# Batched 64x64 matrix multiplication: the second half of six `a` tiles' transposes moved ahead of the multiplication it used to follow

## The chip, the cores and the metric

The kernel runs on one core of a Trainium2 chip. The metric is the device time of one execution in microseconds (us); lower is better. Next to it the profile gives a span, from the first to the last instruction, which is here about 1.8 us shorter than the time.

## The reference, cut to what matters

```python
a = np.random.randn(1024, 64, 64).astype(np.float32)
b = np.random.randn(1024, 64, 64).astype(np.float32)
out = np.matmul(a, b).astype(np.float32)
```

Each of the three tensors has 1024 x 64 x 64 x 4 bytes = 16.8 MB. The kernel reads two of them and writes one, 50.3 MB, each byte once.

## The kernel before

The work is cut into 8 tiles of `a` (index s, 128 products each) and 16 tiles of `b` and of the output (index t, 64 products each); tile t uses half of `a` tile t // 2. The steps concerned here, and the engines that do them:

- `regroup(s)`: VectorE casts and reorders the loaded `a` tile to bf16.
- `transpose(s, j)`: TensorE transposes half j of it (8 transposes), ScalarE copies the results from PSUM, the memory that TensorE writes, into `at_sb` (2 copies).
- `spread(t)`: VectorE spreads `at_sb`, which must hold both halves j, into a block-diagonal matrix `at_bd` (4 copies).
- `cast(t)`: VectorE casts the `b` tile to bf16, `b_bf`.
- `multiply(t)`: TensorE runs 64 matmuls, and ScalarE (for odd t VectorE too) evicts, that is copies, 8 pieces of PSUM into `o_sb` (16 smaller ones of the last tile).
- `store(t)`: GpSimd issues the transfer of `o_sb` to memory, one tile later than its multiplication.

```python
    def transpose(s, j):
        a_cols = abf_tiles[s][:].rearrange("p v h k -> p v (h k)").bitcast(fp32)
        for wl in range(2):
            at_ps = t_psum.tile([128, 4, 128], fp32, name="at_ps")
            for vo in range(4):
                nc.tensor.transpose(
                    at_ps[:, vo, :], a_cols[:, 4 * vo + 2 * j + wl, :], identity[:]
                )
            nc.scalar.copy(
                at_tiles[s][:, j, :, wl, :, :],
                at_ps[:].rearrange("p vo (g mp) -> p g mp vo", mp=4),
            )
    # ... cut: spread, cast, the body of multiply ...
        if last:
            held[t] = [lambda q=q: put(2 * q, 2) for q in range(4)]
        else:
            whole = t < n_t - 2
            held[t] = [lambda q=q: put(q, 8 if whole else 4) for q in ([0] if whole else [0, 4])]
    # ... cut: the start ...
        for t in range(n_t):
            s, half = t // 2, t % 2
            if t + 1 < n_t:
                spread(t + 1)
                cast(t + 1)
            if t + B_AHEAD < n_t:
                load_b(t + B_AHEAD)
            if half == 0 and 0 < s < n_s - 1 - A_AHEAD:
                load_a(s + 1 + A_AHEAD)
            multiply(t)
            if t == 0:
                regroup(1)
                load_a(A_AHEAD)
                load_a(A_AHEAD + 1)
                transpose(1, 0)
            elif t == 1:
                regroup(2)
            elif half == 0 and s + 2 < n_s:
                regroup(s + 2)
            if half == 0 and s + 1 < n_s:
                transpose(s + 1, 1)
            if half == 1 and s + 2 < n_s:
                transpose(s + 2, 0)
            if t >= HOLD - 1:
                store(t - HOLD + 1)
```

The order of these lines is the order in which each engine gets its instructions.

## Time and profile before

| | before |
|---|---|
| time, median of 3 | 135.64 us (135.61 to 135.66) |
| span of the profiled run | 133.8 us |
| busiest compute engine | VectorE, 93.9 us, 70% |
| bytes between memory and core | 50.3 MB, 376 GB/s over the span |
| last eviction ends | 123.67 us |
| VectorE's waits for the transposed copies | 15.1 us in 6 waits |

The profile is read from two sides. The page says which resource is occupied over the whole span. The timeline says what each engine does and, in brackets, how long it had idled before and what ended that. Here is one place of the timeline of the kernel before, with start and duration in us ahead of engine and line: the transposes of the second half on TensorE, and ScalarE around them.

```profile
57.11 1.44 PE L115 MATMUL at_ps<-identity,a_bf 128*128 128x128 f32 x8
...
59.78 0.58 ACT L172 COPY o_sb<-o_ps 64x512 f32<-64x512 f32 x1
...
60.39 1.07 ACT L118 COPY at_sb<-at_ps 128x512 f32<-128x512 f32 x2
...
61.35 3.56 ACT L172 COPY o_sb<-o_ps 64x512 f32<-64x512 f32 x6
```

TensorE is done with the transposes at 58.55. ScalarE copies them out (line 118) only at 60.39, since the evictions (line 172) of the multiplication written before them come first. VectorE's spread, which starts at 61.50, waited for that.

### The profile page before, as it was taken

The numbers are of one execution on the slowest core, as the hardware profiler recorded it, in microseconds if no ns is written. First come the engines' busy times: TensorE is split into PE (matmuls) and PEld (weight loads), VectorE is DVE, ScalarE is ACT, GpSimd is POOL, SyncE is SP. The second block draws the span as 40 slices with busy tenths as digits, with TensorE's granted clock in tenths as the row PEclk, the third lists the DMA queues.
The fourth block names the chain that finished last, engine by engine and source line by source line (L and its number), as shares of the span: only waits on it lengthen the run. The fifth ranks groups of instructions, "written<-read, shape, count | busy, mean of one in ns | idle before, by whom it ended". The sixth has DMA issues, their size and how long they took to land.

```text
span 133.8 us, 2832 instructions
## 1 busy us (share of the span) xinstructions
PE 65.8 (49%) x1152; PEld 61.6 (46%) x1152; DVE 93.9 (70%) x120; ACT 87.7 (66%) x161; POOL 37.4 (28%) x49
## 2 busy tenths in 40 slices
PE   0005505990078524976398276839535860974000
PEld 0005305990078513966396266738525750963000
DVE  5920299208997039998998999999889949979000
ACT  3134504999137994399779979967994999498000
POOL 8981000420082150307023021404200430426400
PEclk9999999999558965589658977977997798555555
DMA  3999999999999999999999999999999999999991
GB/s 75 359 335 312 305 315 312 306 304 305 306 307 384 365 310 310 393 391 396 317 306 355 403 388 371 318 301 374 393 390 391 393 396 404 404 387 356 337 334 51
DMA packets 17485, 45.01 MB, mean 336 GB/s; under 512 B 1088, under 2 KB 1088, under 8 KB 17472
## 3 DMA queue, kind: packets, MB, share of 16 engines
q0 software_dynamic: 7440, 22.28, 54.8%
q1 hardware_dynamic: 5520, 13.11, 27.0%
q10 hardware_dynamic: 4512, 9.44, 18.6%
q8 instruction: 9, 0.15, 0.4%
q14 instruction: 4, 0.03, 0.1%
HBM read 33.55 MB, written 16.78 MB: 376 GB/s over the span
## 4 chain that ended last, share of the span: by engine, by line
DMA 35%; SPq 27%; ACT 10%; issue 8%; DVE 7%; POOL 3%; PE 3%; POOLq 1%; ACTq 1%; DVEq 0%
SPq L72 23%; DMA a_raw<-in_a_dram 18%; DMA b_sb<-in_b_dram 17%; ACT o_sb L172 8%; DVE at_bd L128 4%; SPq L91 3%; POOL out_dram L161 3%; DVE b_bf L139 3%; PE o_ps L184 3%; ACT at_sb L118 2%; SPq L85 1%; ACT b_bf L146 1%; POOLq L277 1%; ACTq L91 1%; POOLq L161 0%
## 5 line engine op out<-in xcount | busy, mean ns | idle before, releaser
L172 ACT COPY o_sb<-o_ps 64x512 f32<-64x512 f32 x106 | 61.6, 581 | 15.6 <-PE o_ps L184 14.4
L184 PEld LDWEIGHTS <-at_bd 128*128 128x128 bf16 x1024 | 42.8, 114 | 38.0 <-DVE b_bf L139 27.3
L184 PE MATMUL o_ps<-b_bf,at_bd 128*128 128x64 bf16 x960 | 41.2, 214 | 33.3 <-DVE b_bf L139 24.5
L128 DVE COPY at_bd<-at_sb 32x1024 f32<-32x1024 f32 x64 | 45.7, 714 | 16.8 <-ACT at_sb L118 15.1
L161 POOL DMA_DIRECT2D out_dram<-o_sb x20 | 20.3, 1018 | 62.0 <-ACT o_sb L172 24.8
L115 PE MATMUL at_ps<-identity,a_bf 128*128 128x128 f32 x128 | 23.2, 346 | 21.9 <-ACT a_bf L100 11.5
L115 PEld LDWEIGHTS at_ps<-identity,a_bf 128*128 128x128 f32 x128 | 19.7, 184 | 22.1 <-issue 19.3
L118 ACT COPY at_sb<-at_ps 128x512 f32<-128x512 f32 x32 | 17.5, 590 | 8.2 <-PE at_ps L115 7.9
L68 POOL DMA_DIRECT2D a_sb<-in_a_dram x21 | 13.0, 634 | 25.2 <-DVE a_bf L103 19.4
L139 DVE CAST b_bf<-b_sb 128x2048 bf16<-128x2048 f32 x14 | 17.9, 1277 | 1.1 <-DMA b_sb<-in_b_dram 0.7
L172 DVE COPY o_sb<-o_ps 64x512 f32<-64x512 f32 x14 | 9.7, 690 | 0.3
L106 DVE CAST a_bf<-a_raw 128x1024 bf16<-128x1024 f32 x7 | 4.8, 687 | 6.3 <-DMA a_raw<-in_a_dram 6.3
L103 DVE COPY a_bf<-a_sb 128x3072 bf16<-128x3072 bf16 x7 | 6.7, 952 | 0.0
L100 ACT CAST a_bf<-o_sb 128x1024 bf16<-128x1024 f32 x2 | 2.1, 1044 | 5.5 <-DMA o_sb<-in_a_dram 5.5
L139 ACT CAST b_bf<-b_sb 128x2048 bf16<-128x2048 f32 x1 | 1.9, 1898 | 4.0 <-DMA b_sb<-in_b_dram 4.0
L100 DVE CAST a_bf<-o_sb 128x1024 bf16<-128x1024 f32 x2 | 2.5, 1249 | 2.6 <-DMA o_sb<-in_a_dram 2.6
L172 DVE COPY o_sb<-at_ps 64x256 f32<-64x256 f32 x8 | 3.4, 422 | 1.0 <-PE at_ps L184 0.9
L184 PE MATMUL at_ps<-b_bf,at_bd 128*128 128x64 bf16 x64 | 3.6, 242 | 1.0 <-DVE at_bd L128 1.0
L212 DVE MEMSET at_bd<- 128x4096 f32 x1 | 3.5, 3472 | 0.8 <-issue 0.8
L172 ACT COPY o_sb<-at_ps 64x256 f32<-64x256 f32 x8 | 2.9, 367 | 0.1
L209 ACT ACT_TABLE_LOAD x1 | 1.3, 1283 | 2.3 <-issue 2.3
L217 POOL MEMSET at_bd<- 128x2048 f32 x1 | 1.8, 1849 | 0.0
(12 smaller groups left out, 5.6 us busy)
## 6 DMA issues: line engine op xcount, KB each, us to landing
out_dram<-o_sb POOLq DMA_DIRECT2D x14, 1024.0 KB, 22.9
a_sb<-in_a_dram POOLq DMA_DIRECT2D x21, 256.0 KB, 17.8
a_raw<-in_a_dram SPq DMA_DIRECT2D x7, 512.0 KB, 24.1
o_sb<-in_a_dram ACTq DMA_DIRECT2D x2, 512.0 KB, 7.4
o_sb<-in_a_dram SPq DMA_DIRECT2D x2, 512.0 KB, 6.3
out_dram<-o_sb POOLq DMA_DIRECT2D x2, 512.0 KB, 9.4
out_dram<-o_sb POOLq DMA_DIRECT2D x4, 256.0 KB, 8.1
b_sb<-in_b_dram SPq DMA_DIRECT2D x8, 0.5 KB, 22.0
```

Of the source, the lines that this page charges most:

```text
L68: nc.gpsimd.dma_start(out=a_sb[:, h, :, :].rearrange("p v k -> p (v k)"), in_=a_v[s, h])
L72: nc.sync.dma_start(out=a_raw[:].rearrange("p v k -> p (v k)"), in_=a_v[s, 3])
L91: queue.dma_start(out=b_sb[:], in_=b_v[t])
L103: nc.vector.tensor_copy(a_bf[:, :, 0:3, :], cast_sb[:].rearrange("p h v k -> p v h k"))
L106: nc.vector.tensor_copy(a_bf[:, :, 3, :], raw[:])
L115: nc.tensor.transpose(at_ps[:, vo, :], a_cols[:, 4 * vo + 2 * j + wl, :], identity[:])
L118: nc.scalar.copy(at_tiles[s][:, j, :, wl, :, :], at_ps[:].rearrange("p vo (g mp) -> p g mp vo", mp=4),)
L128: nc.vector.tensor_copy(bd[rows, :, :, :, h, :].rearrange("p j g wl mo -> p j (g wl) mo"), at_tiles[t // 2][rows, :, half, :, :, :].rearrange(
L139: (nc.vector.tensor_copy if t else nc.scalar.copy)(b_bf[:], b_sb[:])
L161: nc.gpsimd.dma_start(out=o_v[t, :, lo : lo + n, :], in_=o_sb[:, lo : lo + n].rearrange("p gh j wl n -> p (gh j wl n)"),)
L172: copies[2 * par + wl](dst, src)
L184: nc.tensor.matmul(o_ps[:, gl, g % 2, j, :], at_bd[:, j, g, :, u], b_bf[:, g, 64 * u : 64 * u + 64], start=(u == 0), stop=(u == 1),)
```

## The change

The intent is to have the transposed copies ready earlier: for s from 1 to 6 `transpose(s + 1, 1)` is written before `multiply(2s)`, so ScalarE copies it out ahead of that multiplication's eight evictions, and VectorE's next spread has nothing to wait for.

```diff
             if half == 0 and 0 < s < n_s - 1 - A_AHEAD:
                 load_a(s + 1 + A_AHEAD)
+            if half == 0 and 0 < s < n_s - 1:
+                transpose(s + 1, 1)
             multiply(t)
             if t == 0:
                 regroup(1)
                 load_a(A_AHEAD)
                 load_a(A_AHEAD + 1)
                 transpose(1, 0)
+                transpose(1, 1)
             elif t == 1:
                 regroup(2)
             elif half == 0 and s + 2 < n_s:
                 regroup(s + 2)
-            if half == 0 and s + 1 < n_s:
-                transpose(s + 1, 1)
```

## The prediction

> **What bounds the kernel now.** I read the page's busy shares and 40 slices first, then its table of DMA queues, then the timeline, then transfers window by window at the end of the span.
>
> ```profile
> PE 65.8 (49%) x1152; PEld 61.6 (46%) x1152; DVE 93.9 (70%) x120; ACT 87.7 (66%) x161; POOL 37.4 (28%) x49
> ...
> DMA  3999999999999999999999999999999999999991
> ...
> q0 software_dynamic: 7440, 22.28, 54.8%
> q1 hardware_dynamic: 5520, 13.11, 27.0%
> q10 hardware_dynamic: 4512, 9.44, 18.6%
> ...
> HBM read 33.55 MB, written 16.78 MB: 376 GB/s over the span
> ```
>
> No compute engine passes 70% of the span, while the 16 DMA engines show 9 in every slice but the first and last. The three large queues' packet times sum to 54.8 + 27.0 + 18.6 = 100.4% of 16 engines' span: there was a packet in hand practically always. These bytes are fixed: 1024 x 16 KB x 3 tensors = 50.3 MB. So transfers bound the whole, unless they are only busy because compute feeds them exactly as fast as they drain. That I settle at the end of the span, where a bound by compute would show as DMA engines running dry before the last stores.
>
> The chain of waits that ended last puts 35% on DMA and 27% on SyncE's issuing, mostly `a_raw` loads held in the issuer for over 10 us each; that too looks like full queues. But seen from the engines alone, the middle of the kernel looks like VectorE's:
>
> ```profile
> 49.50:61.40 11.90, 8.71 (x145) 8.08 (x145) 11.09 (x15) 7.81 (x16) 2.08 (x2) 0.65 1.05 365
> 61.40:73.40 12.00, 8.17 (x147) 7.54 (x143) 11.22 (x14) 10.22 (x21) 3.86 (x6) 0.72 1.06 337
> 73.40:84.80 11.40, 7.09 (x138) 6.50 (x135) 11.03 (x15) 10.23 (x21) 2.35 (x3) 0.85 1.04 380
> ```
>
> Columns: window, length, then busy time of PE, weight loads, DVE, ACT and POOL, the granted clock, DMA share and GB/s. One `a` tile (two multiplications) takes about 11.8 us, of which VectorE works 11.1. So VectorE paces the computing there, and the change speaks to just that pace.
>
> One `a` tile moves 3 x 2.1 = 6.3 MB. At the 376 GB/s of the page that is 16.7 us, more than the 11.8 us of compute. So in this stretch compute gains on the transfers; loads are ahead, and what lags is stores, held in 8 output buffers. The debt falls due at the end:
>
> ```profile
> 117.00:121.00 4.00, 3.05 (x58) 2.89 (x56) 3.02 (x6) 3.89 (x8) 1.10 (x2) 0.50 1.03 386
> 121.00:125.00 4.00, 0.85 (x16) 0.69 (x13) 2.57 (x7) 2.35 (x7) 3.12 (x5) 0.50 1.01 353
> 125.00:130.00 5.00, 0.00 (x0) 0.00 (x0) 0.00 (x0) 0.00 (x0) 0.15 (x1) 0.50 0.99 334
> 124.00:134.00 10.00, 0.00 (x0) 0.00 (x0) 0.00 (x0) 0.00 (x0) 1.15 (x2) 0.50 0.67 231
> ```
>
> After 124.0 no compute engine does anything; stores alone run for another 8 us or so.
>
> **What the skill says.** The Trainium skill's "DMA: Bandwidth & Descriptors", section "Issuing engines are not separate DMA queues", says that transfers started by any engine end on the same 16 DMA engines and interleave. The sum of 100.4% agrees. "Perfetto Trace Analysis", section "Identifying the Most-Contended Engine", warns that occupancy of 16 DMA engines misleads and asks for HBM utilization; section "Roofline" takes 358 GB/s as a core's share and about 435 GB/s as what the 16 engines of a core alone can do. The measured 376 lies between, 86% of the latter; slices reach 404. So the engines are not at the page's ceiling, and a little better mixing could be worth something, but the queues never empty. "TensorE: Matmul & The Clock Gate", section "Architectural detail: the array is 16× 32×32, not 1× 128×128", says ScalarE and VectorE are strict FIFO and TensorE pulls only weight loads ahead. Hence moving lines really moves execution. The trace agrees: ScalarE's transposed copies at 60.39 us run after the evictions written before them.
>
> **The change, part by part.** It adds and removes no instruction. For s = 1 to 6 it puts 8 PE transposes and their 2 ScalarE copies before multiplication 2s. At t = 0 the two transposes stay adjacent and in their place, so nothing changes there. Moved in all: 48 transposes and 12 copies. A batch of 8 transposes took 1.07 to 1.97 us in the timeline; two copies 2 x 0.59 = 1.18 us (1.07 as merged).
>
> What it should win: after multiplication 2s VectorE goes through spread and cast for 2s+1 and the regrouping of a later tile, then the spread for 2s+2, which needs both halves of the transposed tile. Today the second half is copied behind all eight evictions:
>
> ```profile
> 61.50 2.83 DVE L128 COPY at_bd<-at_sb 32x1024 f32<-32x1024 f32 x4 [0.58 <-ACT at_sb L118]
> ...
> 73.44 2.83 DVE L128 COPY at_bd<-at_sb 32x1024 f32<-32x1024 f32 x4 [0.40 <-ACT at_sb L118]
> ...
> 97.04 2.83 DVE L128 COPY at_bd<-at_sb 32x1024 f32<-32x1024 f32 x4 [0.58 <-ACT at_sb L118]
> ...
> 109.30 3.10 DVE L128 COPY at_bd<-at_sb 32x1024 f32<-32x1024 f32 x4 [1.72 <-ACT at_sb L118]
> ```
>
> The brackets are VectorE's idle time: 0.58 + 0.40 + 0.58 + 1.72 = 3.28 us. At 84.78 there is no such wait, and earlier long ones (15.76, 30.47) belong to tiles that the change doesn't touch. With the copies early, all four should vanish.
>
> What it costs: the 2 copies stand ahead of the eight evictions of 2s. But ScalarE idles there now: 0.93, 3.34, 1.56, 0.95, 1.88 and 1.87 us before the evictions at 41.22, 55.63, 67.57, 78.91, 91.17 and 103.43 in the timeline, waiting for PE. The six holes sum to 10.5 us; the six pairs of copies need 6 x 1.1 = 6.6 and fit nearly everywhere. PE has room as well: it waits 2.0 to 4.0 us for the cast `b_bf` before each even multiplication. So the copies are mostly hidden and computing gains at most 3.3 us, likely 2 to 3. Part of it is doubtful: at 100.54 VectorE waits 0.67 us for a `b` load, so what is won earlier is then in part waited for again.
>
> On the end of the span: from 117 us on the trace moved 4.94 MB. Stores 14 and 15, 2.10 MB, were not yet issued at 117.0 (first piece 118.29). So 4.94 - 2.10 = 2.84 MB were already queued, 7.4 us at that window's 386 GB/s. Compute that comes 3 us earlier adds to a queue that lasts 7 us; **the expected share on the path is nearly nothing**. What can be left is mixing: stores alone ran at 334 GB/s from 125 to 130 us, against a mean of 395 from 100 to 112 us, while loads ran along. If 2 to 3 us of compute turn 1 MB of store from the first to the second, 1.05/0.334 - 1.05/0.395 = 0.49 us; I take half, since loads would be displaced and the slow tail looks tied to the smaller last pieces: 0.24 us. So 135.64 - 0.24 = 135.4 us.
>
> **Rivals.**
> 1. VectorE bounds, and its waits count in full: 135.64 - 3.28 = 132.4 us, 2.4% faster. For it: 11.1 of 11.8 us busy. Against: 2.84 MB queued at 117 us, and 8 us of stores alone after compute.
> 2. A new wait on ScalarE or PE: all six pairs of copies delay evictions in full, 6 x 1.18 = 7.1 us later compute. For it: ScalarE is busy 10.2 of 11.8 us. The queue at the end covers up to about 7 us, so even that gives at most 136 to 137. Against: the holes listed above. A subtler version is the clock: batches of 64 matmuls take 2.04 us after short gaps and 3.59 after long ones, and moving transposes away lengthens the gap before odd multiplications. It costs 1.5 us of PE, which has slack.
> 3. Transfers are hidden anyway and simply reorder: earlier stores compete with loads of `b`, VectorE waits for those. Time stays within 0.5 us of before. This is close to what I predict; it differs in showing growing DMA waits on VectorE.
>
> **Range and chances.** Runs before lie within 0.05 us, so noise is small. Below, rival 1 in part (a third of 3.28 us) gives 134.5; above, a worse packing or delayed loads 0.5 us, to 136.1. Faster by over 2% needs under 132.9, nearly the whole of rival 1: 3%. Slower by over 2% needs over 138.4, more than rival 2 gives: 1%.
>
> **What would show it.** DMA stays at 9 in all middle slices and the queues still sum to about 100%. VectorE's waits for `at_sb` fall by about 3 us from 61 us on; ScalarE's idle before even evictions shrinks by about 1 us each. Compute's last eviction comes 1 to 3 us before the present 123.7, and the time from it to the end grows by as much. I am wrong if the span shrinks as much as compute does (then queued stores weren't the bound), if the GB/s of the tail change by over 5%, or if compute ends later.

## The result, and the profile after

The changed kernel is correct and takes 135.48 us in the median of 4 runs (135.40 to 135.87), beside 135.62 us for the kernel before (135.51 to 135.66). The ratio is 0.9996, with a 95% interval of 0.9976 to 1.0017: the same time. Ratios here and below are the mean time of one kernel's runs over that of the other's runs of the same rounds, so they are not quite the ratios of the medians quoted.

The profiled span is 133.8 us, as before. On the page, the DMA row, the three queues' lines and the bytes are as they were. What changed is inside. The timeline of the changed kernel, at the place that answers to the one shown of before, and at the four spreads that the prediction listed with waits of 0.58, 0.40, 0.58 and 1.72 us:

```profile
48.97 1.97 PE L115 MATMUL at_ps<-identity,a_bf 128*128 128x128 f32 x16 [1.30 <-DVE a_bf L106]
...
50.13 2.05 ACT L118 COPY at_sb<-at_ps 128x512 f32<-128x512 f32 x4
...
54.14 4.74 ACT L172 COPY o_sb<-o_ps 64x512 f32<-64x512 f32 x8 [1.96 <-PE o_ps L184]
...
60.49 2.84 DVE L128 COPY at_bd<-at_sb 32x1024 f32<-32x1024 f32 x4
...
71.89 3.08 DVE L128 COPY at_bd<-at_sb 32x1024 f32<-32x1024 f32 x4
...
95.35 3.21 DVE L128 COPY at_bd<-at_sb 32x1024 f32<-32x1024 f32 x4
...
107.00 3.09 DVE L128 COPY at_bd<-at_sb 32x1024 f32<-32x1024 f32 x4
```

All 16 transposes of a tile now run in one batch, ScalarE copies all four results in one go before the evictions, and none of the four spreads has a bracket any more. The aim of the change is met. Two lines each of the table of waits show what became of it (who waited for whom: us in total, times, longest). The kernel before:

```profile
DVE at_bd L128 <- ACT at_sb L118: 15.1, 6, 6.3
...
DVE b_bf L139 <- DMA b_sb<-in_b_dram: 0.7, 1, 0.7
```

The changed kernel:

```profile
DVE at_bd L128 <- ACT at_sb L118: 11.6, 2, 6.0
...
DVE b_bf L139 <- DMA b_sb<-in_b_dram: 2.6, 4, 1.5
```

VectorE waits 3.5 us less for the copies (the four waits, 3.28 us, are gone; the two that stay belong to the start). It waits 1.9 us more for loads of `b`. So over half of what was won was waited for again, on transfers, in this pair of profiles. In two further pairs told below (whole stores, two queues) the copies gave back 3.7 and 3.0 us, and the waits for `b` grew by 1.1 and 0.5 us only.

One such wait matters most. It stands between the third of the four spreads and the fourth. The kernel before:

```profile
100.54 1.23 DVE L139 CAST b_bf<-b_sb 128x2048 bf16<-128x2048 f32 x1 [0.67 <-DMA b_sb<-in_b_dram]
```

The changed kernel:

```profile
100.06 1.23 DVE L139 CAST b_bf<-b_sb 128x2048 bf16<-128x2048 f32 x1 [1.50 <-DMA b_sb<-in_b_dram]
```

The changed kernel started its third spread 1.69 us ahead of the kernel before (95.35 and 97.04), but this cast only 0.48 us ahead, and the fourth spread 2.30 us ahead (107.00 and 109.30). In the two other pairs the lead at this cast was -0.28 and 0.09 us, and 1.84 and 1.54 us at the fourth spread. So a load of `b` that comes at about 100 us in either order takes back what the earlier moves won, and the lead at the end is the last move's. Of the 1.69 us in the pair shown, 0.73 were there at 48.8 us already, ahead of all four waits, since an `a` load landed earlier (VectorE waited 5.71 us for it and not 6.26); the two other pairs had 0.04 and 0.03 us there.

The end of computing, the last evictions on VectorE and ScalarE. The kernel before:

```profile
120.18 3.49 DVE L172 COPY o_sb<-at_ps 64x256 f32<-64x256 f32 x8 [0.91 <-PE at_ps L184]
120.40 3.03 ACT L172 COPY o_sb<-at_ps 64x256 f32<-64x256 f32 x8
```

The changed kernel:

```profile
117.59 3.49 DVE L172 COPY o_sb<-at_ps 64x256 f32<-64x256 f32 x8 [0.22 <-PE at_ps L184]
118.34 3.03 ACT L172 COPY o_sb<-at_ps 64x256 f32<-64x256 f32 x8
```

Start plus duration gives the end: 123.67 us before, 121.37 us after, 2.3 us sooner in this profile. The windows of the changed kernel that answer to those in the prediction (window, length, busy PE, weight loads, DVE, ACT, POOL, granted share of TensorE's full clock, packets' time as a share of the 16 DMA engines', GB/s):

```profile
117.00:121.00 4.00, 1.49 (x52) 1.37 (x47) 3.67 (x9) 3.86 (x10) 1.77 (x4) 1.00 1.03 384
121.00:125.00 4.00, 0.00 (x0) 0.00 (x0) 0.08 (x1) 0.37 (x1) 1.99 (x3) 0.65 1.00 343
125.00:130.00 5.00, 0.00 (x0) 0.00 (x0) 0.00 (x0) 0.00 (x0) 0.00 (x0) 0.50 0.99 343
```

The compute columns empty earlier, the last two columns stay: a DMA share of 1.03, 1.00 and 0.99, beside 1.03, 1.01 and 0.99 before. The time from the last eviction to the end of the span grew from 10.1 to 12.4 us, by exactly what computing gained.

### The profile page after: what moved, and what is told of

Same layout as the page of the kernel before. It is cut to its first block, busy times and chain, and to the rows that moved or that the text cites. A ratio compares the mean times of both kernels' runs of the same rounds, so it can differ in the third digit from the quotient of the medians.

```text
span 133.8 us, 2832 instructions
## 1 busy us (share of the span) xinstructions
PE 65.7 (49%) x1152; PEld 62.7 (47%) x1152; DVE 94.6 (71%) x120; ACT 87.7 (66%) x161; POOL 38.5 (29%) x49
## 4 chain that ended last, share of the span: by engine, by line
DMA 35%; SPq 27%; DVE 15%; issue 6%; ACT 3%; POOL 3%; PE 3%; POOLq 1%; DVEq 0%; ACTq 0%
SPq L72 22%; DMA a_raw<-in_a_dram 18%; DMA b_sb<-in_b_dram 17%; DVE at_bd L128 8%; DVE b_bf L139 5%; SPq L91 3%; POOL out_dram L161 3%; PE o_ps L184 3%; ACT o_sb L172 2%; DVE o_sb L172 1%; SPq L85 1%; ACT b_bf L146 1%; DVE a_bf L106 1%; DVE a_bf L103 1%; POOLq L278 1%
## 5 line engine op out<-in xcount | busy, mean ns | idle before, releaser
L184 PEld LDWEIGHTS <-at_bd 128*128 128x128 bf16 x1024 | 41.6, 111 | 34.9 <-DVE b_bf L139 22.4
L184 PE MATMUL o_ps<-b_bf,at_bd 128*128 128x64 bf16 x960 | 41.9, 215 | 31.1 <-DVE b_bf L139 20.9
L128 DVE COPY at_bd<-at_sb 32x1024 f32<-32x1024 f32 x64 | 46.0, 719 | 13.4 <-ACT at_sb L118 11.6
L115 PEld LDWEIGHTS at_ps<-identity,a_bf 128*128 128x128 f32 x128 | 21.6, 196 | 20.8 <-issue 19.3
L118 ACT COPY at_sb<-at_ps 128x512 f32<-128x512 f32 x32 | 16.9, 596 | 8.2 <-PE at_ps L115 8.0
L68 POOL DMA_DIRECT2D a_sb<-in_a_dram x21 | 13.9, 673 | 25.9 <-DVE a_bf L103 19.9
L139 DVE CAST b_bf<-b_sb 128x2048 bf16<-128x2048 f32 x14 | 17.4, 1245 | 2.9 <-DMA b_sb<-in_b_dram 2.6
L106 DVE CAST a_bf<-a_raw 128x1024 bf16<-128x1024 f32 x7 | 5.5, 792 | 5.7 <-DMA a_raw<-in_a_dram 5.7
L184 PE MATMUL at_ps<-b_bf,at_bd 128*128 128x64 bf16 x64 | 2.0, 193 | 1.2 <-DVE at_bd L128 1.2
## 6 DMA issues: line engine op xcount, KB each, us to landing
out_dram<-o_sb POOLq DMA_DIRECT2D x4, 256.0 KB, 10.1
```

Of the source, the lines that this page charges most:

```text
L68: nc.gpsimd.dma_start(out=a_sb[:, h, :, :].rearrange("p v k -> p (v k)"), in_=a_v[s, h])
L106: nc.vector.tensor_copy(a_bf[:, :, 3, :], raw[:])
L115: nc.tensor.transpose(at_ps[:, vo, :], a_cols[:, 4 * vo + 2 * j + wl, :], identity[:])
L118: nc.scalar.copy(at_tiles[s][:, j, :, wl, :, :], at_ps[:].rearrange("p vo (g mp) -> p g mp vo", mp=4),)
L128: nc.vector.tensor_copy(bd[rows, :, :, :, h, :].rearrange("p j g wl mo -> p j (g wl) mo"), at_tiles[t // 2][rows, :, half, :, :, :].rearrange(
L139: (nc.vector.tensor_copy if t else nc.scalar.copy)(b_bf[:], b_sb[:])
```

## The experiments

The theory is that transfers set the end: they are in hand all the time, and computing that ends sooner only lengthens the queue of stores. The rivals are that VectorE's chain sets the end and the change gained nothing for it, or that something new took the gain. The first pair lightens the transfers, the delays load the computing, and the last runs look at the tail.

### Less to store: does the order of the transposes matter then?

Tiles 0 to 13 store only half of each tile, in both kernels. The output is wrong (the unwritten half makes the error undefined); computing is untouched.

```diff
-            held[t] = [lambda q=q: put(q, 8 if whole else 4) for q in ([0] if whole else [0, 4])]
+            held[t] = [lambda q=q: put(q, 4) for q in ([0] if whole else [0, 4])]
```

> The kernel before, with only half of each of the first 14 output tiles stored (wrong output on purpose): 14 x 0.52 = 7.3 MB of 50.3 MB less to move, computing untouched. Theory (queued transfers set the end): the time falls well below 135.6 us, to where computing and a short last store set it, about 123 to 127 us (computing now ends at 123.7 of a span of 133.8, and its DMA waits shrink). Rival (VectorE's chain sets the end even now): the time hardly moves, above 133 us.

> The changed kernel with the same half stores. Theory: once transfers no longer set the end, the order of the transposes shows: 1.5 to 3.3 us faster than the kernel before with half stores (computing ended 2.3 us sooner in the changed kernel, 3.28 us of waits on the transposed copies are gone). Rival (what the waits on copies gave is taken back by waits on loads of b or by slower PE batches): within 0.5 us of the kernel before with half stores.

Measured: 130.73 us for the order before (ratio to the kernel before 0.9642, interval 0.9600 to 0.9684) and 127.90 us for the changed order (0.9433, interval 0.9379 to 0.9487). The first lies 3.7 us above the range that I had expected, as computing itself became no faster: its last eviction came at 123.01 us, beside 123.67 with all stores, and the span went on for another 6.8 us of last stores. The second is 2.8 us faster than the first, and the intervals do not touch. So the same change that is worth nothing in the full kernel is worth about 2.2% where transfers leave it room. The DMA and GB/s rows of the 40 slices show that room. The order before with half stores:

```profile
DMA  3999999999999999999999999999999934222790
GB/s 72 357 341 309 309 312 316 307 304 296 320 307 340 334 309 331 390 351 290 319 390 352 311 305 383 393 407 371 347 331 339 335 147 167 77 87 83 249 313 9
```

The changed order with half stores:

```profile
DMA  3999999999999999999999999999999998043790
GB/s 56 361 353 305 306 312 322 306 308 285 317 304 310 375 306 310 374 391 302 293 353 389 336 313 314 385 392 398 396 376 307 365 324 319 4 170 123 243 310 1
```

Toward the end of both rows the DMA engines fall to 0 to 4 tenths before the last stores come. Here the last stores wait for computing. In the full kernel, before and after the change, there is no such dip.

### One of the six moves alone

With half stores and the order before, only `transpose(7, 1)` is moved, ahead of multiplication 12.

```diff
+            if t == 12:
+                transpose(s + 1, 1)
             multiply(t)
...
-            if half == 0 and s + 1 < n_s:
+            if half == 0 and s + 1 < n_s and t != 12:
                 transpose(s + 1, 1)
```

> The kernel before with half stores (wrong output on purpose), and only the last of the six moves made (at tile 12). The kernel before with half stores waited 2.31 us for the copies there and 2.06 us at four earlier places. If the waits add up as they stand, this gains about 2 us of the 2.8 us (128.3 to 129.3 us) and the earlier five moves the rest. If the earlier moves carry the gain, it stays near 130.5 us.

Measured: 128.10 us, ratio 0.946, which can't be told from the 0.9433 of all six moves. So the last move carries nearly the whole gain: 130.73 - 128.10 = 2.6 us by the medians (2.5 us by the ratios, which is the fairer comparison of runs from different rounds and chips), about the 2.31 us for which VectorE had waited there, within the spread of these runs (127.61 to 129.36). What became of the five others can be read from the waits of VectorE. With the last move alone:

```profile
DVE at_bd L128 <- ACT at_sb L118: 13.6, 5, 6.2
...
DVE o_sb L172 <- ACT o_sb L172: 0.6, 1, 0.6
...
DVE b_bf L139 <- DMA b_sb<-in_b_dram: 0.2, 1, 0.2
```

With all six moves:

```profile
DVE at_bd L128 <- ACT at_sb L118: 11.8, 2, 6.2
...
DVE b_bf L139 <- DMA b_sb<-in_b_dram: 1.6, 1, 1.6
DVE o_sb L172 <- ACT o_sb L172: 1.0, 1, 1.0
```

The earlier moves save 13.6 - 11.8 = 1.8 us of waiting for copies, and 1.4 us more are waited for a load of `b`, 0.4 us more for an eviction: 1.8 us again, in these two profiles. The early part of the gain was traded mostly for a transfer even here; the last move comes after that wait, and no load takes it back.

### Computing made later

Idle VectorE memsets of a 128x1024 scratch tile are put into one iteration of the loop, 3 or 10 of them, at tile 13.

```diff
     warm = consts.tile([128, 2], fp32)
+    idle = consts.tile([128, 1024], fp32)
...
             s, half = t // 2, t % 2
+            if t == 13:
+                for _ in range(10):        # 3 in the run with 3
+                    nc.vector.memset(idle[:], 0.0)
```

> The changed kernel with 3 idle VectorE memsets (about 2.6 us by the 3.47 us of the 128x4096 memset) ahead of tile 13's work. Theory: the stores queued at the end hide it, time within 0.4 us of the changed kernel. Rival (the last computing sets the end): 2.6 us slower, about 138.1 us.

> The changed kernel with 10 such memsets, about 8.7 us. Theory: the queue covers some 6 us (last piece landed near 131.9, its issue ended near 123.1, an unqueued piece needs some 2.5 us), so the rest, 2 to 4 us, shows: 137.5 to 139.5 us. Rival: the full 8.7 us, 144 us.

> The kernel before with the same 10 memsets. Theory: it lacks the 2.3 us by which computing ended sooner, and here, where the queue has run dry, that shows: 1.5 to 3 us slower than the changed kernel with 10 memsets. Rival (the change gained nothing that lasts): within 0.5 us of it.

A memset took 0.91 us plus 0.28 us to the next, so 10 of them are 11.9 us and not 8.7. The range expected for 10 was therefore too low: with 11.9 the same sum gives 135.5 + 11.9 - 6 = 141.4 us. Measured: with 3 memsets the changed kernel takes 135.55 us (ratio 0.9997, interval 0.9980 to 1.0014), though its last eviction came at 124.73 us, 3.4 us later than without them and later than in the kernel before. With 10 memsets it takes 140.80 us, and the kernel before with 10 takes 141.06 us. The last eviction with 3 memsets:

```profile
121.24 3.49 DVE L173 COPY o_sb<-at_ps 64x256 f32<-64x256 f32 x8 [0.88 <-PE at_ps L185]
```

The run with 3 is the plainest evidence for the theory: 3.4 us of later computing cost nothing. The other two give a size of what is hidden. In the changed kernel the last eviction moved from 121.37 to 132.93, 11.6 us, and the time rose by 140.80 - 135.48 = 5.3; 6.2 us were hidden. In the kernel before it moved from 123.67 to 133.27, 9.6 us, and the time rose by 141.06 - 135.62 = 5.4; 4.2 us were hidden. The difference of 2.1 us confirms nothing: both sums start from the last evictions without memsets, so the 2.3 us between those are in it by construction. These are sums over single profiles.

The expected gap of 1.5 to 3 us between the two was missed: it is 0.26 us, which lies in the range set down for the rival. The experiment was badly placed: the memsets at tile 13 sit right where VectorE waited 1.72 us for the copies in the kernel before, and filled that wait (its waits for the copies were 12.9 us there and not 15.1). Before that wait there was hardly a lead to show: the memsets started at 107.42 us in the changed order and at 107.76 in the order before. So I put them one tile later.

### The same delay one tile later

```diff
-            if t == 13:
+            if t == 14:
```

> The kernel before with the 10 memsets (11.9 us as measured) one tile later, where they can't fill VectorE's 1.72 us wait ahead of tile 14's spread. Theory: the last eviction moves to about 135.6 us of the span and, with the queue run dry, the span ends some 6 us after it (6.0 and 6.0 in the two first delay runs), so about 143.5 us. Rival (the change gained nothing that lasts, and the 0.26 us between the first two delay runs is all there is): within 0.5 us of the changed kernel with the same delay.

> The changed kernel with the same later memsets. Theory: last eviction near 133.1 us, about 141.1 us in all, 1.8 to 2.7 us faster than the kernel before with them. Rival: within 0.5 us of it.

Measured: 141.03 us for the order before (ratio 1.0408, interval 1.0377 to 1.0440) and 140.55 us for the changed order (1.0349, interval 1.0315 to 1.0384). The expected 143.5 us and the expected difference both failed. The time after the last eviction was 4.4 us and not 6, because tile 14's store had been issued before the delay and only 1 MB was left. And the difference is 0.5 us with intervals that overlap, not 2: in these profiles the memsets started at 114.86 (order before) and 114.71 us (changed order), so at this point the changed kernel had almost no lead at all. As worded, the rival (within 0.5 us) came true in both placings: under these delays the change gained nothing that lasts. That its gain can last where there is room, only the runs with half stores show.

Multiplication 13 shows where the lead had gone. TensorE's timeline has it in the kernel before as

```profile
107.64 2.04 PE L184 MATMUL o_ps<-b_bf,at_bd 128*128 128x64 bf16 x64 [1.24 <-DVE b_bf L139]
```

in the changed kernel as

```profile
107.15 2.45 PE L184 MATMUL o_ps<-b_bf,at_bd 128*128 128x64 bf16 x64 [2.43 <-DVE b_bf L139]
```

and in the changed order with whole last stores (an experiment told below) as

```profile
107.56 3.59 PE L184 MATMUL o_ps<-b_bf,at_bd 128*128 128x64 bf16 x64 [3.20 <-DVE b_bf L139]
```

In five profiles with the transposes in their old place and all stores, this batch of 64 matmuls took 2.04 us, after TensorE had idled 0.45 to 1.35 us. In six with them moved ahead it took 2.45 to 3.60 us, after 2.42 to 3.20 us of idling, as nothing stands between multiplications 12 and 13 there any more; the granted clock from 106 to 112 us was 0.89 to 1.00 in the five of the first kind, and 0.50 to 0.72 in the six of the second. In the changed kernel with the later memsets it took 3.30 us; ScalarE then waited 1.84 us for the first matmuls, and VectorE 1.21 us for ScalarE's evictions of the same tile:

```profile
109.45 3.55 ACT L173 COPY o_sb<-o_ps 64x512 f32<-64x512 f32 x6 [1.84 <-PE o_ps L185]
...
113.04 1.39 DVE L173 COPY o_sb<-o_ps 64x512 f32<-64x512 f32 x2 [1.21 <-ACT o_sb L173]
```

In the order before with these memsets, the spread ahead of them started at 108.80 us and VectorE's eviction at 113.19; here they started at 107.39 and 113.04. So a lead of 1.4 us had shrunk to 0.15. The lead at the last eviction was 2.3, 0.6 and 1.1 us in the three pairs of full kernels profiled (plain, whole stores, two queues). I did not run a kernel that changes the idling alone, so that the idling causes the lower clock is not shown. It fits the run with whole stores, where the clock was 1.00 from 105 to 106 us and 0.50 from 107 on. It does not fit the run with 3 memsets, where the clock was 0.50 from 103 us on, before the idling, and stayed there. Nor is the idle time a measure of the clock: the last batch of the kernel before took 3.59 us after only 0.95 us of idling, that of the same order with two queues 2.04 us after 0.90.

### The tail: whole stores

The last two tiles are stored in one piece of 1 MB each, in both orders.

```diff
-            held[t] = [lambda q=q: put(2 * q, 2) for q in range(4)]
+            held[t] = [lambda: put(0, 8)]
         else:
-            whole = t < n_t - 2
+            whole = True
```

> The changed kernel, with the last two output tiles stored in one piece of 1 MB each instead of 2 x 512 KB and 4 x 256 KB. If small pieces cause the drop of the tail from about 400 to 335-343 GB/s, the last 2.1 MB gain up to 2.1/0.340 - 2.1/0.400 = 0.9 us and the time falls to 134.5-135.0 us. If the drop comes from the queue running out instead, nothing or a loss: 135.4 to 136.5 us, as the last store can only be issued when its whole tile is evicted.

> The kernel before with the same whole last stores. Its computing ends 2.3 us later, but the queue still holds over 5 us of stores then, so by the theory it equals the changed kernel with whole stores within 0.4 us. If it is over 1 us slower than that, the earlier end of computing does have a worth once pieces are large.

Measured: 135.24 us for the changed order (ratio 0.9970, interval 0.9950 to 0.9990) and 135.18 us for the order before (0.9964, interval 0.9947 to 0.9980). Whole stores save about 0.4 us whatever the order of the transposes, which is within 0.1 us the same. But not by the cause that I had named. Windows of the changed order with whole stores:

```profile
117.00:121.00 4.00, 3.26 (x64) 3.15 (x64) 2.74 (x7) 3.86 (x10) 0.89 (x1) 0.58 1.03 387
121.00:125.00 4.00, 0.00 (x0) 0.00 (x0) 1.99 (x5) 0.90 (x3) 0.89 (x1) 0.85 1.01 354
125.00:130.00 5.00, 0.00 (x0) 0.00 (x0) 0.00 (x0) 0.00 (x0) 0.00 (x0) 0.50 0.99 336
```

The rate falls from 387 to 336 GB/s all the same. Small pieces do not make the tail slow.

### The tail: a second queue, and a version that beats both

On top of whole stores, tiles 13 and 15 are stored from SyncE's queue, which by then has nothing to load.

```diff
-            nc.gpsimd.dma_start(
+            (nc.sync if t in (13, 15) else nc.gpsimd).dma_start(
                 out=o_v[t, :, lo : lo + n, :],
```

> The changed kernel with whole last stores, and tiles 13 and 15 stored from SyncE's queue, which has nothing left to load by then. If the drop of the tail to about 340 GB/s belongs to a single queue being left, the 4.9 MB after 117 us go at up to 395 GB/s: 4.9/0.343 - 4.9/0.395 = 1.9 us less, 133.3 to 134.5 us. If the 16 engines bound it whatever the queue: 135.0 to 135.6 us.

> The kernel before with whole last stores and tiles 13 and 15 stored from SyncE's queue, as the changed kernel was run with (134.69 us). Theory (what is queued sets the end, and the order of the transposes is hidden here too): within 0.4 us of that, 134.4 to 135.1 us, so that the 0.9 us are the stores' and none of them the transposes'. Rival (a faster tail uncovers part of the earlier end of computing): 135.2 us or more, as the kernel before with whole stores from one queue (135.18 us).

Measured: 134.69 us for the changed order (ratio 0.9937, interval 0.9913 to 0.9961) and 134.73 us for the order before (0.9927 in five rounds, interval 0.9909 to 0.9944). Both are 0.6 to 0.7% faster than the kernel before. The two orders are equal once more: the 0.9 us are the stores', none of them the transposes'. The changed order gave these windows:

```profile
121.00:125.00 4.00, 0.00 (x0) 0.00 (x0) 0.00 (x0) 0.51 (x2) 0.00 (x0) 0.58 1.03 354
125.00:130.00 5.00, 0.00 (x0) 0.00 (x0) 0.00 (x0) 0.00 (x0) 0.00 (x0) 0.50 1.00 344
```

The rate of the tail is again about 350, so the lack of a second queue is not its cause either, and the expected 1.9 us did not come. Why the rate of stores falls after about 121 us, with all DMA engines busy, stays open. The packets recorded in the trace narrow it a little: in the kernel before the stores' data move in packets of 4096 bytes throughout, and the mean time of one was 165 ns from 112 to 117 us and 192 ns from 125 to 130 us. Each packet takes longer.

## Why the prediction was right

- **What bounds the kernel.** Confirmed. The prediction rested on queues that are never empty and on stores still queued when computing ends. The run with 3 memsets moved computing 3.4 us later at no cost, and half stores moved the time by 4.9 us. Neither agrees with a bound by VectorE.
- **What the change wins in computing.** The four named waits, 3.28 us, vanished, and the holes on ScalarE took the copies, as worked out. The net lead at the end, predicted as 2 to 3 us, was 2.3 us in the profile compared, but only 0.6 and 1.1 us in two other pairs. So it was overestimated; the time did not depend on it.
- **The doubtful part.** That a `b` load would take some of it back was right, and it counted for more than the 0.67 us seen before: with the wait at about 100 us the lead of the earlier moves was gone in all three pairs but for 0.5 us at most.
- **What of it reaches the time.** "Nearly nothing" was right: ratio 0.9996. The 0.24 us set down for better mixing are not confirmed; 0.2% lie inside the interval, and the tail's rate stayed between 334 and 343 GB/s from 125 to 130 us.
- **How much the queue hides.** This size was off. The 7.4 us of queued stores were taken as the time that computing could be late. The delays at tile 13 show 4.2 us for the kernel before and 6.2 us for the changed one; those at tile 14, by the same sum, 5.5 and 8.0 us, so there is no one size. A queue of stores is not all slack, because the last tile's own store still has to be issued and carried after its eviction: with the queue run dry the span ended 6.0 us after the last eviction in the first placing and 4.4 us in the second. For rival 2, 7.1 us of later computing would thus have cost about 2 to 3 us (an estimate: 7.1 - 5.5 and 7.1 - 4.2). The forecast did not hang on this, as computing came earlier and not later.
- **Rival 2's clock.** The slower odd multiplication was foreseen as a mere cost in TensorE's slack. It came, but it is not all slack: in two profiles (whole stores, later memsets) VectorE waited 1.2 us for it through ScalarE at tile 13, most of the lead there. The holes on ScalarE moved as well: those before the even multiplications' evictions shrank from 10.5 to 4.7 us, and new ones of 5.6 us in all opened before the odd ones'. In the time it can't be seen, since the lead can't be seen either. The rival's rule, 2.04 us after short gaps and 3.59 after long ones, has an exception in the very profile that it was read from (3.59 after 0.95 us).
- **Small last pieces.** The remark that the slow tail looks tied to small pieces fell: whole stores leave it at 336 GB/s.
- **Readings that were off.** The 376 GB/s count the bytes of memory (50.3 MB), the GB/s of the slices those of the packets (45.0 MB, 336 on average), since GpSimd loads `a` as bf16, in half the bytes; the two should not be set beside one ceiling. And TensorE's wait before each even multiplication is missing at multiplication 2 (39.46 us). Neither bears on the result.

## What to carry to other kernels

Before an engine's waits are counted as time to be won, look at how much transfer is still queued when the last computation ends, and test it by making computing later on purpose. An order that helps computing is worth having only when transfers leave room: here the same move was worth 2.8 us with less to store and nothing with all of it. A delay meant to measure slack must not stand where the engine would have waited anyway.

## What the Trainium skill lacked or had wrong

- "DMA: Bandwidth & Descriptors": the page has nothing that explains the tail. Stores alone ran at 401 GB/s from 112 to 117 us and at 334 GB/s from 125 to 130 us in the kernel before, with the DMA engines busy in both; pieces of 1 MB (336) or a second queue (344) did not mend it. The section "Issuing engines are not separate DMA queues" lets a second issuer save only the sequencer's time; here two stores from SyncE's queue saved another 0.5 us (135.24 to 134.69, and 135.18 to 134.73 us), in both orders of the transposes. The issue of the last store did end sooner, 0.4 us after the last eviction from SyncE and 1.4 us after it from GpSimd, in both orders; no run here shows whether the 0.5 us are that.
- "TensorE: Matmul & The Clock Gate", section "What's actually happening", has the clock fall after at least one idle window of about 3.4 us. Here, with whole stores and the changed order, a batch of 64 matmuls that followed 3.20 us of idling took 3.59 us, beside 2.04 after 1.24 us in the kernel before, and the granted clock fell within that gap, from 1.00 (105 to 106 us) to 0.50 (107 to 108 us). So the clock fell in a gap shorter than that figure.
